# Packets of 16 KB instead of 8 KB for the cast loads of batches 2 to 15

## The chip, the cores and the metric

The kernel runs on one core of one Trainium2 chip. The metric is the device time of one execution in microseconds (us). Three runs of the kernel before took 203.05, 203.77 and 205.11 us; the median is 203.77 us. The profile is of one execution, with a span of 201.3 us from the first to the last instruction. All times inside the profile count from the start of that span.

## The reference

The input x has 16 batches of 2048 tokens with 256 channels, in fp32. Each token is mixed with the token before it, channel by channel, and two products of the mixed tokens are gated and projected:

```
x_prev[:, 1:, :] = x[:, :-1, :]                      # zero for the first token of a batch
xv = x * time_mix_v + x_prev * (1 - time_mix_v)
xr = x * time_mix_r + x_prev * (1 - time_mix_r)
v  = xv @ value_weight                               # 256 x 256
r  = xr @ receptance_weight                          # 256 x 256
out = (sigmoid(r) * v) @ output_weight               # 256 x 256, fp32 out
```

The reference also computes k from key_weight, but nothing of it reaches the output. So 32 MB of x are read and 32 MB of output are written, both fp32, and three matmuls of 256 x 256 are done per token.

## The kernel before

**Tiling.** A batch is cut into four units of 512 tokens (UB = 4, TU = 512), 64 units in all. The loop over g, from 0 to 62, does one unit per turn; `last_unit` does the last one. Token rows lie on the partitions: partition p of a batch holds 16 consecutive tokens, which are 16 x 256 x 4 bytes = 16 KB of x, contiguous in memory.

**Loads.** `load(b)` (L100 to L109) brings a batch into a tile `x_bf` in bf16. The cast from fp32 happens in the transfer, which is issued from GpSimd's queue (q0 in the profile). Batches 0 and 1 go in pieces of a unit. Batches 2 to 15 go in one transfer each (L109), with an argument that bounds the bytes of one packet on the side that is read. The pool `xpool` has six tiles of one batch. The calls are spread over the loop in `advance` (L415 to L424): batch 2 is asked for at the start, batches 3 to 7 during the units of batch 1, and then batch b + 5 when the transposes of batch b begin. So several loads stand in the queue at a time, and they are carried out in order.

**Transposes.** `transposes(i)` (L188) turns a unit to channels on partitions: TensorE writes `ps_t` in PSUM and ScalarE (ACT) copies it to `xt` (L216). It runs some six units ahead of the unit that is computed (LOOK = 6). For the last 18 units' data (BYDMA = 18) no TensorE transposes are made: `by_dma` (L179, issued at L181) transposes on the SyncE queue instead. The first two of these transfers are told to wait for the last load (`last_load`).

**One unit.** In turn g the order on TensorE is: the r projection of g into `psum_r` (L279), the transposes of a later unit into `ps_t` (L200), the v projection of g into `psum_v` (L279), and the output projection of unit g − 1 into `psum_o` (L303). Each of psum_r, psum_v and psum_o has a single buffer; ps_t has two. ACT does the sigmoid of psum_r (L512), the copy of ps_t into xt (L216) and the copy of psum_o into `o_sb` (L335), in this order in the stage that matters here. VectorE (DVE) scales (L249), adds (L271) and multiplies the gate (L549). GpSimd scales one half of the mixed tokens (L259) and issues the loads. The order on each engine is written out by hand; no scheduler changes it.

**Stores.** `output` (L323) fills a tile `o_sb` of one batch in fp32, 2 MB, in four copies. After every second copy one transfer of 1 MB is issued from SyncE's queue (q1 in the profile). For batches 0 and 1 it is the one at L338, which writes each unit's rows apart, so that one contiguous piece is 4 KB; for later batches it is `store` (L311, issued at L313), with pieces of 8 KB. The pool `opool` (L70) has three buffers. A buffer of it is handed on when everything that reads it is done, so the first copy into the tile of batch b + 3 stands behind both stores of batch b. The first buffer is used at the start for `x_unit`, the first rows of x.

```
xpool = ctx.enter_context(tc.tile_pool(name="xpool", bufs=6))
opool = ctx.enter_context(tc.tile_pool(name="opool", bufs=3))
...
            elif b > 1 and e == 0 and b + 5 < B:
                if b == 2:
                    load(6)
                last_load = load(b + 5)
```

Of the kernel before, what the change touches and what calls it, by code (L numbers as in the profile page):

```python
# [15 lines left out]
def kernel(  # L16
# [25 lines left out]
    nc = tc.nc  # L42
# [37 lines left out]
    x_bf = {}  # L80
# [12 lines left out]
    def rows(b):  # L93
        return x[b].rearrange("(p j) d -> p j d", p=P)

    def unit_rows(t, b, e, n=1):

        return t[b, e * TU : (e + n) * TU, :].rearrange("(e p j) d -> p e j d", p=P, j=UJ)

    def load(b):  # L100
        if b not in x_bf:
            x_bf[b] = xpool.tile([P, J, D], BF16, name="x_bf")
        if b < BYUNIT:
            for e in range(UB):
                nc.gpsimd.dma_start(
                    out=x_bf[b][:, e * UJ : (e + 1) * UJ, :], in_=unit_rows(x, b, e)[:, 0]
                )
            return
        return nc.gpsimd.dma_start(out=x_bf[b], in_=rows(b), max_dma_last_dim=8192)  # L109

    x_unit = opool.tile([P, 3, UJ, D], FP32, name="o_sb")
    tm_rows = consts.tile([2 * KO, P], FP32)
# [1 line left out]
    for m, tm in enumerate([time_mix_r, time_mix_v]):  # L114
        nc.scalar.dma_start(
            out=tm_rows[m * KO : (m + 1) * KO, :], in_=tm.rearrange("(ko p) -> ko p", p=P)
        )
    for h in (1, 0):
        nc.sync.dma_start(
            out=x_unit[:, 0, h * H : (h + 1) * H], in_=unit_rows(x, 0, 0)[:, 0, h * H : (h + 1) * H, :]  # L120
        )
    nc.sync.dma_start(
        out=w_f32[:, 0], in_=receptance_weight.rearrange("(ko p) n -> p ko n", p=P)
# [12 lines left out]
    nc.gpsimd.dma_start(out=x_bf3, in_=unit_rows(x, 0, 3)[:, 0])  # L136
    nc.gpsimd.dma_start(out=wo_bf, in_=output_weight.rearrange("(ko p) n -> p ko n", p=P))
    load(1)
    load(2)

    def warm_up(n):
# [273 lines left out]
    def advance(limit):  # L415
        nonlocal tnext, last_load
        while tnext <= min(limit, NU - 1):
            b, e = divmod(tnext, UB)
            if b == 1 and e > 0:
                load(b + e + 1)  # L420
# [4 lines that stand above are left out]
            if tnext < NU - BYDMA:  # L425
                transposes(tnext)
            tnext += 1

    first_transposes()
    for ko in range(KO):  # L430
        nc.vector.tensor_scalar(
            out=w_prev[:, ko, :],
# [6 lines left out]
        out=w_bf[:, 0, 0, :], in0=w_f32[:, 0, 0, :], scalar1=tms[:, 0, 0:1], scalar2=None, op0=ALU.mult  # L439
    )  # L440
    nc.scalar.activation(
        out=w_bf[:, 0, 1, :], in_=w_f32[:, 0, 1, :], func=ACT.Copy, scale=tms[:, 0, 1:2]
# [3 lines left out]
    for ko in range(KO):  # L446
        nc.vector.tensor_scalar(
            out=w_bf[:, 1, ko, :],
# [141 lines left out]
```

## Time and profile before

| what | value |
|---|---|
| time, median of 3 runs | 203.77 us |
| span of the profiled run | 201.3 us |
| busy: TensorE / VectorE / ScalarE / GpSimd | 97% / 93% / 90% / 41% |
| DMA moved, as written | 56.74 MB, 282 GB/s over the span |
| q0 (loads with cast): packets, share of 16 engines | 4800, 40.5% |
| q1 (stores, first loads, DMA transposes): packets, share | 26160, 59.2% |
| load of a batch (14 of them): issue to landing, median | 27.1 us |
| store of 1 MB (28 at L313): issue to landing, median | 9.5 us |

The busy shares are averages over stages. A busy TensorE in the profile is not TensorE at its peak, but its chain of matmuls can be compared with its own steady pace. The DMA share is the mean over 16 transfer engines that all queues have in common; the bytes of a load are counted as written, so a load that reads 2 MB of fp32 counts as 1 MB of bf16. The time from issue to landing holds the wait behind what was queued earlier, so a long one says that a queue is full and not that the transfer itself is slow.

### The profile page before, as it was taken

How to read it: one execution, taken by the hardware profiler on the slowest of the kernel's cores; microseconds unless marked ns; L12 is line 12 of the kernel's file. 1: busy time of each engine (PE TensorE's matmuls, PEld its weight loads, DVE VectorE, ACT ScalarE, POOL GpSimd, SP SyncE). 2: the span in 40 equal slices, each digit the busy share in tenths (PEclk: the TensorE clock that was granted, in tenths of full speed). 3: DMA queues.
4: the chain of work that ended last, by engine and by line, in shares of the span. 5: the costliest groups of instructions: out<-in, count | busy, mean ns of one | idle time of the engine just before them, and what ended most of it. 6: DMA issues, size and time to landing. Idle time of an engine off the chain costs nothing.

```text
span 201.3 us, 3922 instructions
## 1 busy us (share of the span) xinstructions
PE 195.9 (97%) x1436; PEld 127.1 (63%) x1436; DVE 186.7 (93%) x301; ACT 180.9 (90%) x202; POOL 83.3 (41%) x109
## 2 busy tenths in 40 slices
PE   7999999999999999999999999999999999999992
PEld 7766676666666666666666666665656565555671
DVE  2899999999999999999999999999999999999963
ACT  2699899999999999999999999989999999999982
POOL 1754543462542644434462543434344444444200
PEclk9999999999999999999999999999999999999999
DMA  5999999999999999999999999989999999997575
GB/s 187 282 177 217 237 281 274 276 283 273 298 313 309 315 311 304 291 316 298 289 295 291 300 313 295 300 310 181 297 170 405 241 349 254 280 417 314 212 311 210
DMA packets 31130, 56.74 MB, mean 282 GB/s; under 512 B 19716, under 2 KB 21000, under 8 KB 28040
## 3 DMA queue, kind: packets, MB, share of 16 engines
q1 hardware_dynamic: 26160, 40.24, 59.2%
q0 software_dynamic: 4800, 16.12, 40.5%
q8 instruction: 11, 0.18, 0.3%
q10 hardware_dynamic: 152, 0.13, 0.2%
q14 instruction: 7, 0.06, 0.1%
HBM read 34.34 MB, written 33.55 MB: 337 GB/s over the span
## 4 chain that ended last, share of the span: by engine, by line
PE 83%; ACT 5%; DMA 5%; issue 3%; DVE 2%; SPq 0%; POOL 0%; DVEq 0%; ACTq 0%
PE psum_o L303 25%; PE psum_v L279 24%; PE psum_r L279 24%; PE ps_t L200 8%; DMA x_bf<-in_x_dram 3%; DMA w_f<-n_receptance_weight_dram 2%; ACT s_sb L512 2%; ACT mix L491 1%; ACT o_sb L335 1%; ACT xt L216 1%; DVE mix L271 1%; DVE z_sb L549 1%; DVE mix L249 1%; PE ps_t L303 1%; PE ps_t L279 0%
## 5 line engine op out<-in xcount | busy, mean ns | idle before, releaser
L259 POOL TENSOR_SCALAR mix<-xt,c_sb 128x1024 bf16<-128x1024 bf16 (+1 forms) x55 | 61.0, 1109 | 91.8 <-DVE mix L271 80.9
L549 DVE TENSOR_TENSOR z_sb<-s_sb,psum_v 128x1024 bf16<-128x1024 bf16 x63 | 76.6, 1217 | 3.6 <-PE psum_v L279 1.5
L271 DVE TENSOR_TENSOR mix<-mix,xt 128x1024 bf16<-128x1024 bf16 x112 | 77.3, 698 | 1.7
L279 PEld LDWEIGHTS <-w_bf 128*128 128x128 bf16 x516 | 48.7, 98 | 37.9 <-issue 0.7
L512 ACT ACTIVATE s_sb<-psum_r 128x1024 bf16<-128x1024 f32 x63 | 65.0, 1032 | 3.4 <-PE psum_r L279 2.7
L335 ACT COPY o_sb<-psum_o 128x1024 f32<-128x1024 f32 x60 | 61.1, 1018 | 7.5 <-PE psum_o L303 7.5
L279 PE MATMUL psum_v<-mix,w_bf 128*128 128x512 bf16 (+1 forms) x256 | 65.3, 377 | 0.3 <-DVE z_sb L549 0.2
L303 PE MATMUL psum_o<-wo_bf,z_sb 128*128 128x256 bf16 x494 | 64.4, 272 | 0.1
L279 PE MATMUL psum_r<-mix,w_bf 128*128 128x512 bf16 (+1 forms) x252 | 64.3, 377 | 0.1
L303 PEld LDWEIGHTS <-z_sb 128*128 128x128 bf16 x512 | 49.9, 98 | 20.7 <-issue 1.5
L216 ACT COPY xt<-ps_t 128x1024 bf16<-128x1024 bf16 x38 | 38.7, 1029 | 0.0
L200 PEld LDWEIGHTS <-x_bf 128*128 128x128 bf16 x344 | 22.5, 98 | 9.7 <-POOL xt_first L407 0.7
L200 PE MATMUL ps_t<-ident,x_bf 128*128 128x128 bf16 x344 | 25.7, 219 | 0.2 <-DMA x_bf<-in_x_dram 0.2
L249 DVE TENSOR_SCALAR mix<-xt,c_sb 128x1024 bf16<-128x1024 bf16 (+1 forms) x50 | 22.5, 459 | 0.0
L491 ACT ACTIVATE mix<-xt,c_sb 128x1024 bf16<-128x1024 bf16 x11 | 12.7, 1158 | 0.0
L109 POOL DMA_DIRECT2D x_bf<-in_x_dram x14 | 10.5, 749 | 0.0
L271 DVE TENSOR_TENSOR mix<-mix,xt_first 128x1024 bf16<-128x1024 bf16 x15 | 10.2, 686 | 0.1
L259 POOL TENSOR_SCALAR mix<-xt_first,c_sb 128x512 bf16<-128x512 bf16 x6 | 4.1, 686 | 8.3 <-DVE xt_first L408 8.2
L249 DVE TENSOR_SCALAR mix<-xt_first,c_sb 128x512 bf16<-128x512 bf16 x22 | 6.7, 355 | 0.2
L216 ACT COPY xt_first<-ps_t 128x1024 bf16<-128x1024 bf16 x5 | 5.1, 1029 | 0.0
L144 PE MATMUL ps_t<-zeros 128*128 128x128 bf16 x31 | 3.7, 313 | 1.0 <-DVE zeros L87 1.0
L144 PEld LDWEIGHTS <-zeros 128*128 128x128 bf16 x31 | 3.3, 148 | 1.0 <-DVE zeros L87 1.0
(64 smaller groups left out, 48.4 us busy)
## 6 DMA issues: line engine op xcount, KB each, us to landing
out_dram<-o_sb SPq DMA_DIRECT2D x28, 1024.0 KB, 9.5
x_bf<-in_x_dram POOLq DMA_DIRECT2D x14, 1024.0 KB, 27.1
out_dram<-o_sb SPq DMA_DIRECT2D x4, 512.0 KB, 2.7
out_dram<-o_sb SPq DMA_DIRECT2D x6, 256.0 KB, 2.5
x_bf<-in_x_dram POOLq DMA_DIRECT2D x5, 256.0 KB, 6.9
o_sb<-in_x_dram SPq DMA_DIRECT2D x2, 512.0 KB, 4.8
o_sb<-in_x_dram SPq DMA_DIRECT2D x2, 256.0 KB, 2.9
out_dram<-o_sb SPq DMA_DIRECT2D x3, 128.0 KB, 2.0
```

The costliest lines, as they stand in the source:

```text
L109: return nc.gpsimd.dma_start(out=x_bf[b], in_=rows(b), max_dma_last_dim=8192)
L200: nc.tensor.transpose(out=ps[:, jj], in_=src[:, jj, ko * P : (ko + 1) * P], identity=idn)
L216: nc.scalar.copy(out=xt[b][:, j0 : j0 + UJ], in_=ps)
L249: nc.vector.tensor_scalar(out=mixed(piece)[:, :, ko], in0=xt[b][:, slots(piece), ko], scalar1=c_sb[:, m, ko : ko + 1], scalar2=None, op0=A ...
L259: op = nc.gpsimd.tensor_scalar(out=mixed(piece)[:, :, 1], in0=xt[b][:, slots(piece), 1], scalar1=c_sb[:, m, 1:2], scalar2=1.0, op0=ALU.mul ...
L271: return nc.vector.tensor_tensor(out=mixed(piece), in0=mixed(piece), in1=xt[b][:, slots(piece, 1)], op=ALU.add)
L279: nc.tensor.matmul(out=ps[:, mo, :], lhsT=w_bf[:, m, ko, mo * P : (mo + 1) * P], rhs=mixed((b, m, e * TU + lo, e * TU + hi))[:, :, ko], st ...
L303: nc.tensor.matmul(out=ps[:, slot, :], lhsT=z[:, ko, jj * P : (jj + 1) * P], rhs=wo_bf[:, ko, :], start=(ko == 0), stop=(ko == KO - 1),)
L335: nc.scalar.copy(out=o_sb[b][:, j0 : j0 + UJ, :], in_=ps)
L491: nc.scalar.activation(out=mixed(piece)[:, :, ko], in_=xt[b][:, slots(piece), ko], func=ACT.Copy, scale=c_sb[:, m, ko : ko + 1],)
L512: nc.scalar.activation(out=s_sb, in_=ps_r, func=ACT.Sigmoid)
L549: nc.vector.tensor_tensor(out=z_sb, in0=s_sb, in1=ps_v, op=ALU.mult)
```

## The change

One argument of the transfer in `load` changes. It doubles the bound on the bytes that one packet reads. The row of a partition in a batch has 16 KB, so each partition's row goes in one packet instead of two: 128 packets per load instead of 256, for the 14 loads of batches 2 to 15. Its purpose is fewer and longer packets for the same bytes. Nothing else in the program differs: the same loads are issued at the same places into the same buffers.

```
-        return nc.gpsimd.dma_start(out=x_bf[b], in_=rows(b), max_dma_last_dim=8192)
+        return nc.gpsimd.dma_start(out=x_bf[b], in_=rows(b), max_dma_last_dim=16384)
```

## The prediction

> **What bounds the kernel now.** I read the page first: busy shares, slices and the chain that ended last. Then the engines by stage, the DMA queues by window, and the landing times of single loads and stores.
>
> ```profile
> PE   7999999999999999999999999999999999999992
> DMA  5999999999999999999999999989999999997575
> ```
>
> Both rows are full. The chain of waits is 83% TensorE, and in steady state it repeats one unit of 512 tokens: 0.86 us psum_r, 0.46 ps_t, 0.86 psum_v, 0.87 psum_o, together 3.05 us. So matmuls set the end: 64 units at 3.05 us (2.6 us from 134 us on, where DMA does the transposes) plus some 12 us of start. Nothing that only makes transfers faster can shorten that; but the DMA engines have no room either until the last load lands, so the question is whom the queues make wait.
>
> The change alters how loads (q0) and stores (q1) share those engines. Two windows show the present sharing, 33 to 39 us and 60 to 66 us:
>
> ```profile
> DMA packets 440, 1.68 MB, mean 279 GB/s; under 512 B 31, under 2 KB 31, under 8 KB 440
> q0 software_dynamic: 220, 0.84, 68.6%
> q1 hardware_dynamic: 220, 0.84, 36.9%
> ...
> DMA packets 333, 1.88 MB, mean 313 GB/s; under 512 B 27, under 2 KB 27, under 8 KB 182
> q0 software_dynamic: 166, 0.63, 52.4%
> q1 hardware_dynamic: 166, 1.23, 51.0%
> ```
>
> Columns are packets, MB written, and time as a share of 16 engines. In the first window a load packet reads 8 KB (writes 4) and a store packet is 4 KB, since batches 0 and 1 go out by unit; in the second the store packet has 8 KB. The counts are 1 to 1 both times: the engines alternate by packet, whatever its size. Bytes do not decide it.
>
> The stores of batches 0 and 1 (four, 1 MB each) are the slow ones. The second and the fourth:
>
> ```profile
> L338 SPq DMA_DIRECT2D out_dram<-o_sb x1: 395/395/395, 25.6 to 25.6; - x1
> DMA to landing us min/median/max: 13.8/13.8/13.8
> ...
> L338 SPq DMA_DIRECT2D out_dram<-o_sb x1: 373/373/373, 39.7 to 39.7; - x1
> DMA to landing us min/median/max: 14.8/14.8/14.8
> ```
>
> They land at 25.6 + 13.8 = 39.4 and 39.7 + 14.8 = 54.5 us. What waits for them is the o_sb pool, three buffers of one batch each: a tile is released when all its readers are done, so the first ACT copy (L335) into batch b+3's tile must find both stores of batch b landed (the ACT sequencer has one semaphore wait at L335 per batch, at 76.4 us for the copy at 78.1). Batch 3's first copy starts at 53.7 us, batch 4's (unit 16) here:
>
> ```profile
> 64.69 1.02 ACT L216 COPY xt<-ps_t 128x1024 bf16<-128x1024 bf16 x1
> 65.91 1.01 ACT L335 COPY o_sb<-psum_o 128x1024 f32<-128x1024 f32 x1 [0.20 <-PE psum_o L303]
> 66.82 1.03 ACT L512 ACTIVATE s_sb<-psum_r 128x1024 bf16<-128x1024 f32 x1
> ```
>
> The bracket shows it waits for TensorE only: the buffer has been free for 65.9 − 54.5 = 11.4 us. Batch 3 has 53.7 − 39.4 = 14.3 us spare.
>
> **What the skill says.** The Trainium skill, "DMA: Bandwidth & Descriptors", Queues, rings and completion order: each DMA engine goes round robin over its queues and drains a whole packet before it switches. The 220 to 220 and 166 to 166 above agree. Its section SWDGE vs HWDGE vs iDMA prefers packets of at most 4096 B as the switching boundary; the trace has 8 KB packets that alternate as one, and nothing here shows 16 KB on q0. "TensorE: Matmul & The Clock Gate", Part 1: after an idle window of about 3.4 us the TensorE clock falls to half, until some 3.4 us of work. No such idle stretch is in this trace.
>
> **The change, part by part.**
>
> Removed: half of the load packets, 14 loads x 128 = 1,792. No engine issues them one by one: the 14 issues stay 0.75 us each on GpSimd, whose mix scaling starts 1 to 2 us after it is free, waiting for VectorE. Worth nothing on the path.
>
> Cost of a packet. In the first window 96 us of engine time (16 x 6) hold about (440 − 31)/2 = 204 data packets of each kind (the 31 small ones mark completions). Load: 68.6% x 96 / 204 = 0.322 us. Store of 4 KB: 36.9% x 96 / 204 = 0.173 us. A pair advances in 96/204 = 0.470 us, 0.95 of the sum 0.495, as neighbours overlap. From 4 to 8 KB costs 0.149 us, so 16 KB is 0.322 + 2 x 0.149 = 0.620 us, an estimate. The other bound is the page's row "q8 instruction: 11, 0.18, 0.3%": packets of 16 KB at 0.3% x 16 x 201.3 / 11 = 0.88 us. They are another kind of fetch, so I take 0.620.
>
> Moved: the shares. After the change a 4 KB store packet alternates with a 16 KB load packet; a pair takes 0.95 x (0.620 + 0.173) = 0.753 us, 0.283 us more than now. Each of 16 engines has 16 such packets per 1 MB store, 64 for the four. If loads are waiting throughout, the second store lands at 39.4 + 32 x 0.283 = 48.5 us, still 5 us before batch 3's copy. The fourth lands at 54.5 + 64 x 0.283 = 72.6 us, which is 6.7 us after batch 4's copy wants its buffer.
>
> Are loads waiting all that time? A load is 8 packets per engine, 6.0 us at this rate. Load 2 lands at 23.4 us (10.1 + 13.3), before the stores matter much. Then load 3 ends near 27.5 and eight later loads would each take 6 us: load 10 near 69.5, load 11 after that. They are issued at 24.9 us or earlier up to load 7, then 32.7 (8), 42.7 (9), 54.4 (10), 66.4 (11), each ahead of its turn. So yes, q0 stays full until about 76 us.
>
> The added wait: ACT stands 6.7 us before L335 of unit 16. Queued behind it are the sigmoid of unit 18, the xt copy of unit 24 and the next o_sb copy. TensorE still does psum_r, ps_t and psum_v of unit 18, then needs the single psum_o buffer. Its next output matmuls start at 67.9 us now; the copy would end at 66.9 + 6.7 = 73.6 us, so TensorE stands 5.7 us. That is past an idle window of the clock page: half speed for up to 3.4 us costs up to 1.7 us; the phase is free and ACT paces part of the restart, so I take 1.0. Nothing gives it back: ACT is idle 0.2 us a unit afterwards and TensorE not at all.
>
> Is there a second stall? From 72.6 us about five packets of load 11 remain beside 8 KB store packets, 0.95 x (0.620 + 0.322) = 0.89 us a pair, 4.5 us. Load 12 comes only at 78.6 + 5.7 = 84.3. The other 11 packets of batch 2's two stores then go alone at 0.31 us (window 174 to 180 us: 103.1% x 96 / 319), 3.4 us, landing at 80.5. Batch 5 wants that buffer at 78.1 + 5.7 = 83.8. No stall. Later a batch needs 8 x 0.620 + 16 x 0.31 = 9.9 us of each engine in 12.2 us. Enough.
>
> Faster loads: batch 3's transposes start at 32.2 us with its load in at 30.9 already, and the SyncE queue's 2.6 us wait for the last load before the DMA transposes goes, but TensorE lacks only 0.10 us of 130 to 140 us. At most 0.3 us; left out of the sum.
>
> Sum: 203.8 + 5.7 + 1.0 = 210.5 us.
>
> **The rivals.**
>
> *No store waits (14%): 203.6 us.* The engines split a 16 KB packet, or share by bytes beyond 8 KB; stores land as now, and TensorE runs as before, with 0 to 0.3 us won from earlier loads. For it: 11.4 us of spare. Against it: the two windows, where doubling the store packet left 1 to 1. Not slower; the other side of my forecast.
>
> *A small stall (14%): 206 us.* If the pair costs 0.70 instead of 0.753, the fourth store lands at 54.5 + 64 x 0.23 = 69.2, a stall of 3.3 us, 2.3 on TensorE, no clock loss.
>
> *16 KB packets cost more than in proportion (11%): near 228 us.* At 0.88 us the pair is 1.00, 0.53 more: the second store lands at 56.4 (stall 2.7), the fourth at 88.4 against 68.6, some 20 us more, then a little for batch 5. For it: only the q8 row; against: 4 and 8 KB lie on a line with 0.024 us of fixed cost.
>
> **How the numbers follow.** The main case, a stall of 5 to 9 us on ACT, has 61% and gives 210.5. With the small stall and no stall the range reaches 203.3 to 214.5; left out are most of the heavy case and a few points below. Slower by over 1% (above 205.8): main, heavy and nearly all of the small stall, 0.84; within 1%: 0.12; faster: 0.04.
>
> **What would show it.** A new row of waits, ACT o_sb L335 released by the DMA out_dram<-o_sb, once, 6 to 7 us near 66 us; a dip of TensorE's slices at 68 to 74 us; q0 with 1 to 1 counts but four times the bytes read of q1 before 70 us; the fourth store landing 33 us after issue (now 14.8); load landing under 15 us from 80 us on; the last-load wait of SyncE gone. Wrong if q0 still shows 8 KB reads, if a 16 KB packet takes far from 0.62 us, or if q1 gets two packets for each of q0. If the stall is there but the end does not move, the step from ACT to TensorE failed.

## The result, and the profile after

The changed kernel takes 210.37 us (median of 6 runs, 209.27 to 211.86) against 203.78 us (6 runs, 203.05 to 205.11). The ratio is 1.0312, 95% interval 1.0258 to 1.0366: slower by 6.6 us. The forecast was 210.5 us.

The profile of after has a span of 208.3 us. Its slices show one hole in TensorE's work:

```profile
PE   7899999999999199999999999999999999999992
...
PEclk9999999999999969999999999999999999999999
DMA  4999999999999999999999999949999999987575
```

TensorE falls to a tenth in one slice of 5.2 us, its clock dips in the next, and the DMA engines are full in both. So TensorE stood once, while the DMA engines were busy. The table of waits (engine and line, whom it waited for: us in total, times, longest) names the link on each side of ACT:

```profile
ACT o_sb L335 <- PE psum_o L303: 7.0, 31, 0.7
...
ACT o_sb L335 <- DMA out_dram<-o_sb: 6.0, 1, 6.0
PE psum_o L303 <- ACT o_sb L335: 4.7, 1, 4.7
```

The second and third rows are not in the kernel before. The store that is waited for is the fourth of batches 0 and 1, issued at L338:

```profile
L338 SPq DMA_DIRECT2D out_dram<-o_sb x1: 373/373/373, 40.2 to 40.2; - x1
...
  ACT o_sb L335: 6.0, 1
...
DMA to landing us min/median/max: 31.9/31.9/31.9
```

It lands at 40.2 + 31.9 = 72.1 us (54.5 before), and ACT's copy of unit 16 starts then. The timeline of ACT:

```profile
65.20 1.02 ACT L216 COPY xt<-ps_t 128x1024 bf16<-128x1024 bf16 x1
72.17 1.01 ACT L335 COPY o_sb<-psum_o 128x1024 f32<-128x1024 f32 x1 [5.96 <-DMA out_dram<-o_sb]
```

TensorE in the same stretch:

```profile
67.53 1.03 PE L279 MATMUL psum_v<-mix,w_bf 128*128 128x512 bf16 x4
73.24 1.86 PE L303 MATMUL psum_o<-wo_bf,z_sb 128*128 128x256 bf16 x8 [4.68 <-ACT o_sb L335]
74.89 1.87 PE L279 MATMUL psum_r<-mix,w_bf 128*128 128x512 bf16 x4
76.60 0.61 PE L200 MATMUL ps_t<-ident,x_bf 128*128 128x128 bf16 x8
77.05 1.03 PE L279 MATMUL psum_v<-mix,w_bf 128*128 128x512 bf16 x4
```

Two losses can be read here. It stands for 4.68 us, and then eight output matmuls take 1.86 us where they take 1.04, and four of psum_r take 1.87 where they take 1.03: close to half speed. From one psum_v to the next it is 77.05 − 67.53 = 9.52 us instead of 3.05: 6.47 us lost in this turn, nearly the whole difference. The multiplies of the gate (L549) show it for every unit: against before they come some 0.5 us later up to unit 17 (the start of this run was that much later), 6.99 us at unit 19, and 7.00 us at unit 62.

The sharing that caused it, in the window from 33 to 39 us:

```profile
DMA packets 280, 1.53 MB, mean 255 GB/s; under 512 B 32, under 2 KB 32, under 8 KB 155
q0 software_dynamic: 141, 1.02, 81.7%
q1 hardware_dynamic: 139, 0.50, 22.2%
```

Still one packet of each in turn. But stores got 0.50 MB through in 6 us instead of 0.84, and loads 1.02 MB (as written) instead of 0.84.

### The profile page after: what moved, and what is told of

Same layout as the page of the kernel before. It is cut to its first block, busy times and chain, and to the rows that moved or that the text cites. A ratio compares the mean times of both kernels' runs of the same rounds, so it can differ in the third digit from the quotient of the medians.

```text
span 208.3 us, 3922 instructions
## 1 busy us (share of the span) xinstructions
PE 197.2 (95%) x1436; PEld 126.5 (61%) x1436; DVE 186.5 (90%) x301; ACT 181.1 (87%) x202; POOL 80.2 (38%) x109
## 4 chain that ended last, share of the span: by engine, by line
PE 60%; DMA 18%; ACT 10%; DVE 6%; issue 4%; SPq 0%; DVEq 0%; ACTq 0%
PE psum_o L303 19%; PE psum_r L279 18%; PE psum_v L279 17%; DMA out_dram<-o_sb 15%; PE ps_t L200 5%; ACT s_sb L512 3%; ACT o_sb L335 2%; DMA w_f<-n_receptance_weight_dram 2%; DVE mix L271 2%; DVE mix L249 2%; ACT mix L491 2%; ACT xt L216 1%; PE psum_r L293 1%; ACT xt_first L216 1%; DVE z_sb L549 1%
## 5 line engine op out<-in xcount | busy, mean ns | idle before, releaser
L549 DVE TENSOR_TENSOR z_sb<-s_sb,psum_v 128x1024 bf16<-128x1024 bf16 x63 | 76.6, 1216 | 10.1 <-ACT s_sb L512 6.2
L335 ACT COPY o_sb<-psum_o 128x1024 f32<-128x1024 f32 x60 | 61.1, 1018 | 13.1 <-PE psum_o L303 7.0
L303 PE MATMUL psum_o<-wo_bf,z_sb 128*128 128x256 bf16 x494 | 65.2, 275 | 4.8 <-ACT o_sb L335 4.7
L279 PE MATMUL psum_r<-mix,w_bf 128*128 128x512 bf16 (+1 forms) x252 | 65.1, 381 | 0.1
L200 PEld LDWEIGHTS <-x_bf 128*128 128x128 bf16 x344 | 22.4, 98 | 10.2 <-POOL xt_first L407 0.7
L271 DVE TENSOR_TENSOR mix<-mix,xt_first 128x1024 bf16<-128x1024 bf16 x15 | 10.2, 684 | 0.1
L109 POOL DMA_DIRECT2D x_bf<-in_x_dram x14 | 8.1, 576 | 0.0
L144 PE MATMUL ps_t<-zeros 128*128 128x128 bf16 x31 | 3.1, 283 | 1.0 <-DVE zeros L87 1.0
L209 ACT CAST xt_first<-ps_t 128x512 bf16<-128x512 f32 x4 | 2.1, 588 | 1.5 <-PE ps_t L200 1.5
```

The source lines that it names most:

```text
L200: nc.tensor.transpose(out=ps[:, jj], in_=src[:, jj, ko * P : (ko + 1) * P], identity=idn)
L271: return nc.vector.tensor_tensor(out=mixed(piece), in0=mixed(piece), in1=xt[b][:, slots(piece, 1)], op=ALU.add)
L279: nc.tensor.matmul(out=ps[:, mo, :], lhsT=w_bf[:, m, ko, mo * P : (mo + 1) * P], rhs=mixed((b, m, e * TU + lo, e * TU + hi))[:, :, ko], st ...
L303: nc.tensor.matmul(out=ps[:, slot, :], lhsT=z[:, ko, jj * P : (jj + 1) * P], rhs=wo_bf[:, ko, :], start=(ko == 0), stop=(ko == KO - 1),)
L335: nc.scalar.copy(out=o_sb[b][:, j0 : j0 + UJ, :], in_=ps)
L549: nc.vector.tensor_tensor(out=z_sb, in0=s_sb, in1=ps_v, op=ALU.mult)
```

## The experiments

Each run's ratio is to the kernel before, run on the same chip.

**Four buffers.** It takes away the wait and leaves the packets:

```
-    opool = ctx.enter_context(tc.tile_pool(name="opool", bufs=3))
+    opool = ctx.enter_context(tc.tile_pool(name="opool", bufs=4))
```

> The changed kernel with four o_sb buffers instead of three. Theory (the loss is the wait of the copy of unit 16 for the fourth store): the buffer of batch 4 is a fresh one and batch 5 gets the buffer of batch 1 some 12 us later, at about 78 us, when the store (72 us) has landed. The wait of L335 for a DMA is gone though the fourth store still lands near 72 us; the time is 203.8 us, at best 0.3 us under the kernel before. Rival (16 KB packets cost time by themselves, or delay something else): it stays near 210 us.

Measured: 203.54 us, ratio 0.9998 (0.9984 to 1.0013). The fourth store is as late as in the changed kernel, and the copy of unit 16 does not care. The store:

```profile
L338 SPq DMA_DIRECT2D out_dram<-o_sb x1: 372/372/372, 40.7 to 40.7; - x1
DMA to landing us min/median/max: 32.1/32.1/32.1
```

And ACT's copy in its timeline:

```profile
66.96 1.01 ACT L335 COPY o_sb<-psum_o 128x1024 f32<-128x1024 f32 x1 [0.20 <-PE psum_o L303]
```

It lands at 72.8 us, and the copy starts at 66.96 after waiting for TensorE alone. (The pool hands its buffers out in turn and `x_unit` takes the first, so the buffer of batch 4 is here the one of batch 0, not a fresh one; both stores of batch 0 had landed by 48.4 us.) So 16 KB packets by themselves cost no time that can be measured, and the whole loss goes through this buffer. The other half of this pair is the kernel before with four buffers.

> The kernel before, 8 KB, with four o_sb buffers. The fourth buffer's own effect: no copy waits for a store in the kernel before, so 203.8 us, no difference.

Measured: 203.69 us, ratio 1.0005 (0.9988 to 1.0022). The fourth buffer alone changes nothing that can be measured.

**Which loads.** The bound is made to depend on the batch; the kernels differ in the condition only (b <= 6, b <= 8, b <= 9, b >= 9):

```
-        return nc.gpsimd.dma_start(out=x_bf[b], in_=rows(b), max_dma_last_dim=16384)
+        return nc.gpsimd.dma_start(out=x_bf[b], in_=rows(b), max_dma_last_dim=16384 if b <= 6 else 8192)
```

> Packets of 16 KB for the loads of batches 2 to 6 alone, 8 KB for 7 to 15. Theory (the fourth store is late by 0.28 us for each of its queue's packets that alternates with a 16 KB packet): about 32 pairs at 0.753 us up to 48 us, then 32 at 0.47, so the fourth store lands at 63 us, before the copy wants its buffer at about 66: no wait, 203.8 us. Rival (each 16 KB load costs its share, 5 of 14): 206.2 us.

> Packets of 16 KB for the loads of batches 2 to 9, 8 KB for 10 to 15. Theory: 16 KB pairs until about 67 us, by when some 58 of the 64 packets are out; the rest at 0.47 us, so the fourth store lands near 70 us. The wait of ACT is 3.8 us instead of 6.0, TensorE stands about 2.8 us, too short for the clock to fall; 206.6 us. Rival (what costs is the number of 16 KB loads, 8 of 14): 207.6 us and no difference in kind; or, if the wait is not what costs, no relation of the time to the wait.

> Packets of 16 KB for the loads of batches 2 to 8. One load less than in the run with 2 to 9 means 8 pairs at 0.47 instead of 0.753 us: the fourth store lands 2.3 us earlier than there, near 68 us. Theory: the wait of ACT is 2.1 us, TensorE stands 1.3 us less than ACT, so 0.8 us, and is not idle long enough for its clock to fall: 204.4 us. Rival (the loss goes with the number of 16 KB loads, a straight line through 5 loads with none and 8 with 5.1 us): 206.9 us.

> Packets of 16 KB for the loads of batches 9 to 15 alone, 8 KB for 2 to 8. Theory: until load 9 begins, near 70 us, everything is as in the kernel before and the fourth store has landed at 54.5 us; the later stores have 8 KB packets, a pair takes about 0.93 us, and the store before batch 5's copy lands before 80 us as now. Later stores land up to 3 us later each, with more than 10 us to spare. No wait of L335 for a DMA, 203.6 us. Rival (half of the 16 KB loads, half of the loss): 206.8 us.

| 16 KB for loads | fourth store lands | ACT waits | TensorE stands | time, ratio |
|---|---|---|---|---|
| none (before) | 54.5 us | 0 | 0 | ratio 1 |
| 9 to 15 | 55.7 | 0 | 0 | 203.71 us, 1.0002 (0.9983 to 1.0022) |
| 2 to 6 | 64.7 | 0 | 0 | 203.70 us, 1.0013 (0.9993 to 1.0033) |
| 2 to 8 | 67.6 | 2.06 | 0.78 | 204.59 us, 1.0043 (1.0026 to 1.0061) |
| 2 to 9 | 70.2 | 4.34 | 3.07 | 208.58 us, 1.0255 (1.0224 to 1.0285) |
| 2 to 15 (the change) | 72.1 | 5.96 | 4.68 | 210.37 us, 1.0312 (1.0258 to 1.0366) |

The loss is no share per load. Five 16 KB loads cost nothing, since they use up the spare time of the buffer; each load more adds about 2 us to the store's time from issue to landing (23.7, 28.0 and 30.3 us for loads up to 6, 8 and 9); and the seven loads from 9 on do no harm alone, because the fourth store is out before they begin. The rival straight lines fail where they were far from the theory: 206.2 us for loads 2 to 6, 206.9 for 2 to 8, 206.8 for 9 to 15. For loads 2 to 9 the rival's 207.6 us was nearer to the measured 208.58 than my 206.6, so that run by its time alone does not decide between them; its wait does. TensorE stands 1.27 to 1.28 us less than ACT waits, in all three kernels. With loads 2 to 8, ACT:

```profile
67.69 1.01 ACT L335 COPY o_sb<-psum_o 128x1024 f32<-128x1024 f32 x1 [2.06 <-DMA out_dram<-o_sb]
```

And TensorE:

```profile
66.94 1.03 PE L279 MATMUL psum_v<-mix,w_bf 128*128 128x512 bf16 x4
68.75 1.03 PE L303 MATMUL psum_o<-wo_bf,z_sb 128*128 128x256 bf16 x8 [0.78 <-ACT o_sb L335]
```

Full speed after a short stop: eight output matmuls in 1.03 us, and 0.9 us lost in the end. For loads 2 to 9 the wait was 4.34 us against 3.8 expected, but the time was missed by more, 208.6 us instead of 206.6. There the clock did fall. TensorE in that kernel:

```profile
71.36 1.87 PE L303 MATMUL psum_o<-wo_bf,z_sb 128*128 128x256 bf16 x8 [3.07 <-ACT o_sb L335]
73.02 1.52 PE L279 MATMUL psum_r<-mix,w_bf 128*128 128x512 bf16 x4
```

And its windows from 66, 70 and 74 us (length, busy, instructions, granted clock, DMA share, GB/s):

```profile
66.00:70.00 4.00, 2.30 (x18) 1.00 1.04 285
70.00:74.00 4.00, 2.64 (x11) 0.58 1.04 317
74.00:78.00 4.00, 4.00 (x36) 1.00 1.04 316
```

I had held 2.8 us to be too short for that. Standing 3.07 us was enough. A granted clock of 0.58 in the middle window, with 1.00 on both sides, is 0.42 x 4 / 0.5 = 3.4 us at half clock, all of it between 70 and 74 us. So it began by 70.6 us, no more than 2.3 us after TensorE had stopped (71.36 − 3.07 = 68.29). The turn lost 7.56 − 3.05 = 4.51 us, 1.44 more than TensorE stood.

**Loads asked for later.** All packets are 16 KB and there are three buffers; only the times at which loads 7 to 10 are issued change, so that q0 is empty for a while before the first copy of batch 4. In the kernel before, loads 6 and 7 are both asked for when the transposes of batch 2 begin, as the lines taken out show:

```
-                if b == 2:
-                    load(6)
-                last_load = load(b + 5)
+                for n in {2: [6], 3: [7], 4: [8], 5: [], 6: [9, 10, 11]}.get(b, [b + 5]):
+                    last_load = load(n)
```

> The changed kernel, 16 KB packets and three o_sb buffers, with loads 7 to 10 asked for one batch later or more (7, 8 one batch later each, 9 and 10 together with 11 at the sixth batch). Theory (a store packet is held up only while loads wait): loads end near 61 us and q0 is empty until about 70; some 50 of the 64 store packets are out by then and the other 14 go alone at 0.17 us, so the fourth store lands near 63 us: no wait of L335 for a DMA, 203.8 us. Rival (16 KB packets slow the stores as such): stays near 210 us.

Measured: 203.36 us, ratio 0.9991 (0.9971 to 1.0011), no wait of L335 for a DMA. The DMA queues from 63 to 69 us:

```profile
DMA packets 351, 2.54 MB, mean 423 GB/s; under 512 B 38, under 2 KB 38, under 8 KB 44
...
q1 hardware_dynamic: 351, 2.54, 101.3%
```

And the fourth store:

```profile
L338 SPq DMA_DIRECT2D out_dram<-o_sb x1: 372/372/372, 40.0 to 40.0; - x1
DMA to landing us min/median/max: 24.0/24.0/24.0
```

The last load before that window, that of batch 8, landed at 43.0 + 18.9 = 61.9 us. From then on the stores had the engines alone, and the fourth landed at 64.0 us. So it takes both: long load packets, and a queue of loads that doesn't run dry before the fourth store is out.

**The other way, 4 KB.** `max_dma_last_dim=4096` for all 14 loads.

> Load packets that read 4 KB, half of the kernel before, the other way. Theory: a pair of 4 KB packets takes about 0.33 us, so a store of batches 0 and 1 drains in some 5 us and is no longer held up: the fourth lands near 47 us instead of 54.5, and the loads are later instead: load 3 near 31 us, a load every 9.5 us after it. Batch 3's transposes start at 32 us, so this is just in time: 203.8 us, up to 1 us more if load 3 comes late. Rival (fewer and larger packets are better or worse as such): faster or slower by the 1,792 x 2 packets' fixed cost, 0.02 us each over 16 engines, 5 us of engine time.

Measured: 204.02 us, ratio 1.0026 (1.0002 to 1.0051), about a quarter of a per cent slower; in the profiled run the first unit was 0.7 us late already, and nothing was added after unit 5. The fourth store landed at 40.5 + 10.2 = 50.7 us, earlier as expected, but not at 47. The reason is in the window from 33 to 39 us:

```profile
q0 software_dynamic: 411, 0.81, 71.4%
q1 hardware_dynamic: 221, 0.84, 37.0%
```

Here 1.86 load packets go by for each store packet, and not one. That the turns are one to one holds for the 8 and 16 KB load packets, not for these. An equal share of the bytes written would fit this window (0.81 and 0.84 MB), but not the second window of the prediction (0.63 and 1.23 MB). Why is open; no run was made on it.

**The clock alone.** In the changed kernel, TensorE is kept busy while it would stand, with 88 matmuls of zeros into a ps_t tile:

```
+        if g == 18:
+            warm_up(88)
         if z_prev is not None and not LATE_O <= g < NU - 3:
             output(g - 1, z_prev)
```

> The changed kernel with 88 extra matmuls of zeros (128 x 128) on TensorE ahead of the output matmuls of unit 17, that is in the stretch in which it stands still. They change no result. Theory: the wait of ACT stays 6.0 us, but TensorE is not idle for more than about 1 us, its clock is not cut to half for 3.4 us after the wait, and the 1.65 us that this cost in the changed kernel are won back: 208.7 us. Rival (the clock cut is hidden behind ACT's restart): 210.4 us.

Measured: 209.68 us, ratio 1.0305 (1.0277 to 1.0332). TensorE:

```profile
68.10 5.08 PE L144 MATMUL ps_t<-zeros 128*128 128x128 bf16 x88
73.17 1.03 PE L303 MATMUL psum_o<-wo_bf,z_sb 128*128 128x256 bf16 x8
74.09 1.02 PE L279 MATMUL psum_r<-mix,w_bf 128*128 128x512 bf16 x4
```

The half speed is gone, and by unit 25 the gate's multiply is 5.15 us late against before (start taken off) instead of 6.47, though ACT waited 6.18 us for the store here and not 5.96. But the end is late by 5.7 us: at unit 42 some 0.7 us were lost and 0.2 regained. The total can't be told apart from the changed kernel's: the intervals of the two ratios overlap. So the clock's share is read from two traces and is not shown in the time of the whole kernel. I took the exchange of the two ps_t buffers for the cause, and put one more dummy matmul in turn 30 to exchange them back.

> The kernel with 88 extra matmuls of zeros in the stretch in which TensorE stands, and one more in turn 30, so that the two ps_t buffers are again used by the same transposes as in the changed kernel after that. Theory: the 0.7 us that the kernel with 88 alone lost near 141 us came from the exchanged ps_t buffers; without it the loss against the kernel before is 5.3 us: 208.9 us. If the exchanged buffers had no part in it, 209.6 us.

Measured: 210.08 us, ratio 1.0310 (1.0278 to 1.0342). The 0.7 us at unit 42 are still there, so the exchanged buffers were not their cause. In both kernels the first DMA transpose of batch 11 lands 7.0 and 7.1 us after its issue, at 143.8 and 144.7 us, and GpSimd's scaling of that batch starts right then; in the changed kernel it lands at 144.1, before its 144.5. So a TensorE that is earlier by 1.3 us may have run into that transfer. This is read from the traces and was not tried.

## Why the prediction was right

**Sharing by packet, and the price of 16 KB.** Right. In two windows of after, 33 to 39 and 60 to 66 us, the loads wrote 1.02 and 0.98 MB in packets that write 8 KB each, so 125 and 120 packets, in 81.7% and 78.3% of 96 us: 0.63 us a packet both times; 0.620 was estimated. The step of 0.149 us for 4 KB more went from a store packet to a load packet, which was a guess; the 4 KB load packets above took 0.173 us too, like the store's, so it holds. Between the second store's landing (48.0) and the fourth's (72.1) lie 32 pairs, 0.75 us each, as estimated. The heavy rival (0.88) is out, and so are the rival in which engines split a packet and the one with a pair of 0.70 us, which had the fourth store at 69.2 us.

**The landing and the wait.** 72.1 us for 72.6. The wait was 5.96 us for 6.7: the store was 0.5 us earlier, and this run started 0.5 us later, so that the copy wanted its buffer later.

**From ACT to TensorE.** The link was right: psum_o, once, as unit 17's output. It stood 4.7 us for 5.7. The prediction subtracted 1.0 us for the matmuls that TensorE still has; the runs show 1.28, the rest is the shorter wait.

**The clock.** The term was 1.0 us; 6.47 − 4.68 = 1.79 us were lost beside the standing, 1.66 of it in the matmuls at half speed (1.86 − 1.04 and 1.87 − 1.03). The Trainium skill, "TensorE: Matmul & The Clock Gate", Part 1, gives a window of about 3.4 us for both directions. The half speed in the trace fits that, some 3.4 us of work from 73.24 to 76.6. The idle side was shorter here: with loads 2 to 9 the clock fell at most 2.3 us after TensorE had stopped, and in the changed kernel only as TensorE went on (granted clock 0.90 from 70 to 74 us and 0.68 from 74 to 78, so 0.8 and 2.6 us at half, from 73.2 us on), 4.6 us after it had stopped at 68.56. So the time from the stop to the fall differs; the prediction had called the phase free. In the changed kernel all of the half clock fell on work, and the loss was near the 1.7 us that the prediction had as its upper bound; with loads 2 to 9 a part of it passed while TensorE stood. The six times of the changed kernel fit a loss that varies: the three runs with a mean granted clock of 0.992 took 209.27 to 210.09 us, the three with 0.981 to 0.988 took 210.65 to 211.86; only one of the six has a trace. So this term was 0.8 us too small and the one before 1.0 us too large. That their sum, 6.5 us, came out near 6.7 is luck.

**No second stall.** Right, by less than was worked out. Batch 2's second store was put at 80.5 us and landed at 52.2 + 31.9 = 84.1; batch 5's copy came at 85.1. The loads were later than the sum had them: load 3 landed at 30.2 us and not near 27.5, the next seven took 6.5 us each and not 6.0, so load 10 landed at 54.9 + 20.9 = 75.8 us and not near 69.5, and load 11 stood beside those stores until 66.9 + 16.3 = 83.2. (In the kernel before, load 7 was issued at 25.6 us, not by 24.9 as the prediction read it; that changes nothing here.) In the kernel with the 88 extra matmuls, this copy came at 83.8 us and waited 0.56 us for that store.

**Edits costed at nothing.** The 14 issues on GpSimd did not stay at 0.75 us; they fell to 0.58. The other half of the argument holds: it is not on the path, as the run with four buffers shows. The last-load wait of SyncE (2.6 us) is gone and gives no time: with the stall removed, the two ways to keep 16 KB packets measure 0.9998 and 0.9991, no gain that can be measured. Load landing fell to 12.6 us for the load issued at 85.6 and 9.8 for the one at 122.2, and TensorE had no use for it. No version here is measurably faster than the kernel before.

## What to carry to other kernels

When two queues share the DMA engines and both are full, the size of a packet in one can set the share of the other (here it did for load packets of 8 and 16 KB), so a longer packet on a load that is early anyway can hold up a store that is not. Ask of every transfer on the other queue how long its buffer has been free before it is wanted (here 11.4 us), how many packets stand between, and multiply by what each now waits longer. If longer packets are wanted, one more buffer or a later issue of loads gives back that time; where TensorE sets the end, neither is a gain.

## What the runs showed of the hardware

A packet of these casting loads took engine time nearly in proportion to what it reads: 0.173 us for 4 KB (71.4% of 96 us for 0.81 MB in pieces of 2 KB written, 396 packets), 0.322 us for 8 and 0.63 us for 16. A store packet of 4 KB took 0.173 us too, half of what a load packet takes that writes 4 KB. GpSimd's issue of the same 1 MB load got shorter with fewer packets: 0.797, 0.751 and 0.577 us (medians) for 512, 256 and 128 packets. TensorE's clock fell to half when it stood for 3.07 us, within 2.3 us of the stop, and did not when it stood for 0.78 us; with the half speed it lost 1.4 to 1.8 us beyond the standing.
